# Two rounded TensorE products in place of an fp32 one for the partition sums of eight modulation blocks

## The chip, the core and the metric

The kernel runs on one core of a Trainium2 chip. The metric is the device time of one execution in microseconds (us); the median of several runs counts. TensorE is called PE below (PEld is its weight load), VectorE DVE, ScalarE ACT, GpSimd POOL; SP, the sync engine, only issues DMAs here.

## What is computed

A two-layer diffusion backbone over 2048 latent tokens and 256 context tokens, model width 1024. Every layer is modulated by a condition vector:

```python
def modulation(cond, w, b):
    m = jnp.dot(jax.nn.silu(cond), w) + b
    return jnp.split(m[..., None, :], 3, axis=-1)      # shift, scale, gate

for i in range(DEPTH):                                  # DEPTH = 2
    shift, scale, gate = modulation(c, ada_w[i], ada_b[i])
    c_shift, c_scale, c_gate = modulation(c_ctx, ada_w[i], ada_b[i])
    h = rms_norm(x, norm_g[i]) * (1 + scale) + shift
    hc = rms_norm(cx, norm_g[i]) * (1 + c_scale) + c_shift
    ...
```

Layer 0 is a latent attention beside a gated linear attention, layer 1 a neighbourhood attention. The modulation is a product of two condition vectors (latent and context) with a 1024 x 3072 matrix for each layer. Cut into columns of 512, that is six blocks for each layer: blocks 0 and 1 are the shift, 2 and 3 the scale, 4 and 5 the gate.

## The kernel before

**Numbers as pairs.** Most products on PE are of `float32r` operands. A value is split into a part `hi`, rounded to `float32r`, and the rest `lo`, and a product is three PE instructions: hi by hi, hi by lo, lo by hi (`mm3`). ACT makes `hi` by a copy, DVE makes `lo` by a subtraction.

**Stages.** `even_latent` runs over 18 tiles of 128 tokens. For tile `s` it normalises and modulates the input (`prep`: PE transposes L335 into the tile `px`, ACT scales them into `x`, DVE makes `hhi` and `hlo`), multiplies by three pieces of a weight matrix (`gemm`: W0, W1, W2, 24 PE instructions of 352 columns each, tile `gm`), and brings the result to SBUF as `u` (ACT). One tile later `up` transposes `u` on PE (L499, two groups of four into the tile `tp`), splits it into `lth` (ACT) and `ltl` (DVE), and makes queries, keys and values from it (`WU`, `wkv`). Another tile later `fin` transposes these (L554) and stores them. `even_rest` goes on with the remaining weight columns and row maxima of the attention scores, `even_mix` holds the attentions, `odd_*` is layer 1.

**The modulation.** `ada_first` makes blocks 0 to 3 of layer 0 at the start. The eight others (4 and 5 of layer 0, all six of layer 1) come from `ada_steps`, a generator that `even_latent` advances once for each tile from the third on, and twice at two tiles. For a block, DVE multiplies eight weight tiles `adaw` with the two conditions and adds them into the tiles `acc` (named `adac`, 128 x 512, one for each condition; L280 for the first weight tile, L282 for the other seven). The sum over the 128 partitions is then left to PE: at L287 an fp32 product with `pick`, a 128 x 2 matrix with a column of ones, puts the sum for condition `c` into row `c` of a PSUM tile `ps`. `ada_row` adds the bias on DVE (L296, into the tile `adab`) and, for the shift and scale of layer 1 (blocks 0 to 3), transposes the two rows with four small PE products (L301) into a second PSUM tile, from which DVE writes `modB` (L304) or `modA` (L306). Gates are stored to memory instead.

**Buffers.** The tag `adaw` has two SBUF buffers in `ada_steps`, so that a weight tile's DMA waits until DVE has read the tile before the last. `tp` has two PSUM banks; the modulation's two PSUM tiles share them with the transposes L499 and L554. `gm` and `u` have two buffers each.

**Order.** Each engine runs its instructions in a fixed order, written when the program is built: a scheduler places every instruction on its engine by its own estimate of when the operands are there. An instruction that waits holds up everything behind it on its engine. A small edit can thus move many instructions that it doesn't touch.

Of the kernel before, what the change touches and what calls it, by code (L numbers as in the profile page):

```python
# [11 lines left out]
F32R = mybir.dt.float32r  # L12
AF = mybir.ActivationFunctionType
ALU = mybir.AluOpType
# [3 lines left out]
P = 128  # L18
# [70 lines left out]
class Kern:  # L89
# [119 lines left out]
    def consts(self, es):  # L209
        nc = self.nc  # L210
        self.cp = self.pool(es, "const")
        cp = self.cp
        self.ident = self.tl(cp, [P, P], "ident")
        make_identity(nc, self.ident[:])
        self.mtwos = self.tl(cp, [P, 64], "mtwos")
        nc.gpsimd.memset(self.mtwos[:], -2.0)
        self.mhalf = self.tl(cp, [P, 8], "mhalf")
        nc.gpsimd.memset(self.mhalf[:], -0.5)
        self.ng = self.tl(cp, [P, 2, KD], "ng")
        nc.sync.dma_start(self.ng[:], self.i["norm_g"])  # L220
        self.modA = [self.tl(cp, [P, KD, 2], f"modA{l}") for l in range(2)]
        self.modB = [self.tl(cp, [P, KD, 2], f"modB{l}") for l in range(2)]
        self.condT = self.tl(cp, [P, KD, 2], "condT")
        cond = self.tl(cp, [P, KD, 2], "cond")
        nc.sync.dma_start(cond[:], self.i["cond"])
        th = self.tl(cp, [P, KD, 2], "condth")
        self.act(th[:], cond[:], AF.Tanh, scale=0.5)
        nc.vector.scalar_tensor_tensor(out=th[:], in0=th[:], scalar=1.0, in1=cond[:], op0=ALU.add, op1=ALU.mult)
        nc.vector.tensor_scalar(out=self.condT[:], in0=th[:], scalar1=0.5, scalar2=None, op0=ALU.mult)
        self.pick = self.tl(cp, [P, 2, 2], "pick")  # L230
        nc.gpsimd.memset(self.pick[:], 0.0)
        for c in range(2):
            nc.gpsimd.memset(self.pick[:, c, c : c + 1], 1.0)
        self.gates = self.scr("gates", (2, 2, D), F32)
        self.H = self.scr("H", (2, NT, P, D), F32)

# [33 lines left out]
    def ada_steps(self, jobs, sp, pp, tag):  # L270

        nc = self.nc
        for l, b in jobs:
            acc = [self.tl(sp, [P, 512], f"adac{c}", bufs=1) for c in range(2)]
            for k in range(KD):
                w = self.tl(sp, [P, 512], "adaw", bufs=2)
                nc.sync.dma_start(w[:], self.i["ada_w"][l, :, b, k, :])
                for c, a in enumerate(acc):
                    if k == 0:
                        nc.vector.tensor_scalar(out=a[:], in0=w[:], scalar1=self.condT[:, k, c : c + 1], scalar2=None, op0=ALU.mult)  # L280
                    else:
                        nc.vector.scalar_tensor_tensor(out=a[:], in0=w[:], scalar=self.condT[:, k, c : c + 1], in1=a[:],  # L282
                                                       op0=ALU.mult, op1=ALU.add)
            yield
            ps = self.tl(pp, [P, 512], tag, bufs=2)
            for c, a in enumerate(acc):
                nc.tensor.matmul(ps[:2, :], self.pick[:, c, :], a[:], start=c == 0, stop=c == 1)  # L287
            self.ada_row(l, b, ps, sp, pp, tag)
            yield

# [1591 lines left out]
```

## Time and profile before

| | us |
|---|---|
| runs | 3614.48, 3615.36, 3619.56 |
| median | 3615.36 |
| profiled execution | 3617.2 |
| its span, from the first to the last instruction | 3615.4 |
| mean granted PE clock | 0.988 |

The span is what the profile's views cover; the 1.8 us around it belong to no instruction. A group row of the profile reads: line, engine, operation, output <- inputs, shapes, count, then busy us and the mean ns of one, and the idle time of the engine just before them with what ended it. A row of the timeline reads: start us, duration us, engine, line, operation, and in brackets the idle time before it and what ended it. A row of the windows reads: from:to, length, then busy us and count of each engine, the granted PE clock as a share of full speed, the share of the DMA engines and GB/s.

### The profile page before, as it was taken

What the parts mean: (1) busy time and instruction counts of PE and PEld (TensorE: products, weight loads), DVE (VectorE), ACT (ScalarE), POOL (GpSimd) and SP (SyncE); (2) the same over time, 40 slices, a digit from 0 to 9 for tenths busy, and PEclk for the clock granted to TensorE, in tenths of its full rate; (3) what the DMA queues carried; (4) which work ended last, traced back from release to release, by engine and by line L of the source; (5) the groups of instructions that cost most, each with busy time, mean ns of one, the idle gap of its engine ahead of it and who ended that gap; (6) DMA issues with size and microseconds to landing.
All of it is one profiled execution on the core that took longest, in us unless ns stands there. A gap on an engine that the chain in (4) does not pass through costs nothing. (4 is left out here: it accounts for less than half of the span.)

```text
span 3615.4 us, 51630 instructions
## 1 busy us (share of the span) xinstructions
PE 3523.6 (97%) x18260; PEld 2734.3 (76%) x18260; DVE 2372.3 (66%) x4876; ACT 1430.5 (40%) x2705; POOL 1212.6 (34%) x1342
## 2 busy tenths in 40 slices
PE   8999999999999999999999999999999999999899
PEld 6988998888886666656667878888788886555577
DVE  4677665888886776787664345444587874667721
ACT  5544551111115555555653134444422223555510
POOL 1433430111011232212312233333334444677743
PEclk9999999999999999999999999999999999999999
DMA  7555463222233343334534544456643437888654
GB/s 253 149 153 159 141 191 99 87 77 84 75 109 89 83 104 83 94 92 129 163 91 143 162 164 127 145 143 199 212 139 123 139 122 202 213 213 222 185 178 146
DMA packets 396683, 513.62 MB, mean 142 GB/s; under 512 B 61229, under 2 KB 275197, under 8 KB 390522
## 3 DMA queue, kind: packets, MB, share of 16 engines
q1 hardware_dynamic: 353242, 418.68, 40.0%
q0 software_dynamic: 20192, 56.97, 5.6%
q10 hardware_dynamic: 22992, 34.68, 2.8%
q8 instruction: 145, 2.38, 0.3%
q14 instruction: 112, 0.92, 0.1%
HBM read 330.61 MB, written 179.59 MB: 141 GB/s over the span
## 5 line engine op out<-in xcount | busy, mean ns | idle before, releaser
L1007 DVE TENSOR_TENSOR acc<-acc,apt 128x512 f32<-128x512 f32 x512 | 376.4, 764 | 150.6 <-ACT apt L106 147.0
L666 DVE TENSOR_REDUCE mm<-mx 128x1 f32<-128x512 f32 (+1 forms) x656 | 392.7, 627 | 90.6 <-PE mx L665 82.3
L106 ACT ACTIVATE apt<-st 128x512 f32<-128x512 f32 (+1 forms) x592 | 342.9, 593 | 269.0 <-PE st L1018 229.5
L958 PE MATMUL av<-apt,av 128*64 128x512 f32 (+1 forms) x1184 | 269.2, 592 | 0.0
L1016 PE MATMUL st<-aq,akh 97*128 97x512 f32 x576 | 246.8, 428 | 0.2 <-ACT apt L106 0.2
L665 PE MATMUL mx<-mk,mq 96*128 96x512 f32 (+1 forms) x656 | 238.5, 372 | 0.0
L1017 PE MATMUL st<-aq,akh 96*128 96x512 f32 x576 | 229.1, 398 | 0.0
L1018 PE MATMUL st<-aq,akl 96*128 96x512 f32 x576 | 228.5, 397 | 0.0
L1450 DVE CUSTOM_DVE_ANT_1 mx<-mx,mtab 128x465 f32<-128x465 f32 (+14 forms) x576 | 183.9, 338 | 47.2 <-PE mx L1444 34.5
L106 ACT ACTIVATE u<-gm 128x352 f32<-128x352 f32 (+1 forms) x144 | 70.3, 495 | 358.5 <-PE gm L131 207.7
L106 ACT ACTIVATE opt<-opt 128x930 f32<-128x930 f32 (+9 forms) x144 | 119.2, 830 | 234.5 <-POOL opt L1748 137.0
L958 PEld LDWEIGHTS av<-apt,av 128*64 128x64 f32 x1184 | 79.9, 137 | 152.0 <-issue 150.0
L1708 DVE TENSOR_TENSOR opt<-st,tab 128x64 f32<-128x64 f32 (+10 forms) x576 | 143.0, 314 | 78.3 <-PE st L1548 44.7
L1583 POOL TENSOR_TENSOR oacc<-oacc,opt 128x682 f32<-128x682 f32 (+9 forms) x144 | 173.9, 1230 | 37.8 <-ACT opt L106 36.6
L1016 PEld LDWEIGHTS st<-aq,akh 97*128 97x128 f32 x576 | 109.0, 189 | 72.7 <-issue 44.2
L665 PEld LDWEIGHTS mx<-mk,mq 96*128 96x128 f32 x656 | 122.7, 188 | 11.7
L1018 PEld LDWEIGHTS st<-aq,akl 96*128 96x128 f32 x576 | 110.2, 191 | 25.5
L1017 PEld LDWEIGHTS st<-aq,akh 96*128 96x128 f32 x576 | 110.6, 192 | 17.8
L106 ACT ACTIVATE x<-px,modB,modA 128x128 f32<-128x128 f32 x272 | 99.1, 468 | 58.5 <-PE px L335 39.5
L1547 PE MATMUL st<-q,kt 128*128 128x480 f32 (+5 forms) x256 | 98.7, 388 | 20.2 <-DVE opt L1708 14.8
L129 PE MATMUL gm<-w0h,hhi 128*128 128x512 f32 x288 | 115.3, 400 | 2.3 <-DVE hhi L347 2.3
L129 PE MATMUL gm<-w1h,hhi 128*128 128x512 f32 x288 | 116.7, 405 | 0.0
(584 smaller groups left out, 9906.5 us busy)
## 6 DMA issues: line engine op xcount, KB each, us to landing
q<-Q SPq DMA_DIRECT2D x48, 512.0 KB
H<-x ACTq DMA_DIRECT2D x36, 512.0 KB
adaw<-ada_w SPq DMA_DIRECT2D x64, 256.0 KB
x<-H SPq DMA_DIRECT2D x32, 512.0 KB
K1t<-okt POOLq DMA_DIRECT2D x32, 512.0 KB, 6.7
kt<-K1t SPq DMA_DIRECT2D x32, 512.0 KB
mtab<-rpb_q SPq DMA_DIRECT2D x16, 899.0 KB
QT<-qkhl SPq DMA_DIRECT2D x36, 384.0 KB
```

The source lines that it names most:

```text
L106: return self.nc.scalar.activation(out, in_, func, **kw)
L129: self.nc.tensor.matmul(out, lh(k), rh(k), start=j == 0, stop=False)
L665: mm = nc.tensor.matmul(ps[:, :w], q[:A_QK, (t % 6) * P : (t % 6) * P + P], k[:A_QK, k0 : k0 + w], start=True, stop=True)
L666: nc.vector.tensor_reduce(out=m[:, t, n : n + 1], in_=ps[:, :w], axis=AX.X, op=ALU.max)
L958: nc.tensor.matmul(O[j, nb][i * 64 : i * 64 + 64, :w], V[j, kt // TT][:, kt % TT, i * 64 : i * 64 + 64], pts[i][:, :w], start=n == 0, stop ...
L1007: self.add = nc.vector.tensor_tensor(out=acc[i][:, :w], in0=a[:, :w], in1=pts[i][:, :w], op=ALU.add)
L1016: nc.tensor.matmul(ps[:, :w], kh[: A_QK + 1, i, kq], qh[: A_QK + 1, :w], start=True, stop=False)
L1017: nc.tensor.matmul(ps[:, :w], kh[:A_QK, i, kq], ql[:A_QK, :w], start=False, stop=False)
L1018: mm = nc.tensor.matmul(ps[:, :w], kl[:A_QK, i, kq], qh[:A_QK, :w], start=False, stop=True)
L1450: nc.vector.tensor_tensor_reduce(out=s, in0=s, in1=tb[:, ri : ri + rn, ci : ci + cn], scale=1.0, scalar=-3e38, op0=ALU.add, op1=ALU.max, a ...
L1583: self.psum = nc.gpsimd.tensor_tensor(out=a, in0=a, in1=pts[:, :, a0 - r0 : a1 - r0, :], op=ALU.add)
L1708: nc.vector.tensor_tensor(out=pt[:, d[0], d[1]], in0=ps[:, d[0], d[1]], in1=tabs[j][i][:, ri : ri + rn, ci : ci + cn], op=ALU.add)
```

## The change

A `float32r` copy of `pick` is made at the start by ACT. For each of the two accumulated tiles of a block, ACT copies the values into a `float32r` tile `hi`, DVE subtracts to get the rest `lo`, and two `float32r` products with `pickr`, one of `hi` and one of `lo`, take the place of the fp32 product. The four products of a block add up in the same PSUM tile as before. `hi` and `lo` take the tag `adaw` and so its two buffers: for a block, `hi` and `lo` of condition 0 take both, and those of condition 1 take them again.

```diff
@@ consts
             nc.gpsimd.memset(self.pick[:, c, c : c + 1], 1.0)
+        self.pickr = self.tl(cp, [P, 2, 2], "pickr", F32R)
+        self.act(self.pickr[:], self.pick[:])
@@ ada_steps
             ps = self.tl(pp, [P, 512], tag, bufs=2)
             for c, a in enumerate(acc):
-                nc.tensor.matmul(ps[:2, :], self.pick[:, c, :], a[:], start=c == 0, stop=c == 1)
+                hi, lo = [self.tl(sp, [P, 512], "adaw", F32R, bufs=2) for _ in range(2)]
+                self.act(hi[:], a[:])
+                nc.vector.tensor_tensor(out=lo[:], in0=a[:], in1=hi[:], op=ALU.subtract)
+                nc.tensor.matmul(ps[:2, :], self.pickr[:, c, :], hi[:], start=c == 0, stop=False)
+                nc.tensor.matmul(ps[:2, :], self.pickr[:, c, :], lo[:], start=False, stop=c == 1)
             self.ada_row(l, b, ps, sp, pp, tag)
```

## The prediction

> **What bounds the kernel now.** I read the page first, then the busy time by stretches, then what PE waits for in the stretch where the eight blocks lie, then the timeline around single instructions. The page:
>
> ```profile
> span 3615.4 us, 51630 instructions
> PE 3523.6 (97%) x18260; PEld 2734.3 (76%) x18260; DVE 2372.3 (66%) x4876; ACT 1430.5 (40%) x2705; POOL 1212.6 (34%) x1342
> ```
>
> PE is busy for 97% of the span. The instructions of L287, the partition sums, lie between 119.7 and 445.3 us, and the windows show that PE is as busy there and less so just behind:
>
> ```profile
> L287 PE MATMUL tp<-adac,pick x32: 591/592/593, 119.7 to 445.3; 128*2 128x512 f32 x32
> ...
> 110.00:450.00 340.00, 332.26 (x2006) 304.62 (x2005) 248.17 (x468) 174.94 (x427) 137.14 (x254) 0.99 0.52 152
> 450.00:533.50 83.50, 80.18 (x494) 76.62 (x492) 56.30 (x102) 48.10 (x97) 29.23 (x44) 1.00 0.61 178
> 533.50:561.00 27.50, 23.12 (x115) 20.32 (x116) 8.31 (x13) 8.52 (x12) 1.34 (x2) 0.93 0.87 234
> ```
>
> PE is idle for 7.7 of the 340 us, DVE is busy for 73%, ACT for 51%. So in this stretch a microsecond of PE work that goes away is a microsecond of time, unless PE comes to wait. What it waits for now is nearly always DVE:
>
> ```profile
> PE up L122 <- DVE ltl L502: 4.0, 5, 1.8
> PE tp L499 <- DVE modA L306: 2.0, 1, 2.0
> PE tp L554 <- DVE qkhl L561: 0.9, 1, 0.9
> ```
>
> **The PE work of a block.** The timeline at the first block:
>
> ```profile
> 119.44 0.33 PE L122 MATMUL gm<-W1h,hlo 128*128 128x352 f32 x1
> 119.69 1.88 PE L287 MATMUL tp<-adac,pick 128*2 128x512 f32 x4
> 121.50 0.44 PE L499 MATMUL tp<-ident,u 128*128 128x128 f32 x2
> ```
>
> Durations of PE overlap, so starts are what counts. Two fp32 products are recorded as four passes. A 352-column product makes way for the next after 0.16 us (start to start in a row of them), so without the sums L499 could have started at 119.60; it starts at 121.50. The sums take 1.90 us. Their replacement is four float32r products over 512 columns, for which the products with `wkv` are the row: they follow each other at (191.54 - 191.07) / 2 = 0.235 us.
>
> ```profile
> 191.07 0.39 PE L120 MATMUL up<-wkvh,lth 128*128 128x512 f32 x1
> 191.30 0.39 PE L121 MATMUL up<-wkvl,lth 128*128 128x512 f32 x1
> 191.54 0.39 PE L122 MATMUL up<-wkvh,ltl 128*128 128x512 f32 x1
> ```
>
> 4 x 0.235 = 0.94 us, a saving of 0.96 a block and 8 x 0.96 = **7.7 us** in all. Bounds: a loss of as much as the sums take now, 8 x 1.90 = 15.2 us, if the doubled number of products ran at the fp32 pace of 0.95; a saving of 15.2 if they cost nothing. I take the row, which has the same operand type and moving size.
>
> **The work it adds elsewhere.** For each block two ACT copies and two DVE subtractions of 128 x 512:
>
> ```profile
> L348 DVE TENSOR_TENSOR hlo<-x,hhi 128x512 fp32r<-128x512 f32 x26 | 17.8, 684 | 0.2
> L106 ACT ACTIVATE lth<-tp 128x512 fp32r<-128x512 f32 x25 | 14.9, 598 | 30.7 <-PE tp L499 30.6
> ```
>
> 16 x 0.684 = 10.9 us on DVE and 16 x 0.598 = 9.6 us on ACT, with 92 and 165 us free in the stretch. As load that is hidden by PE's products; if all of DVE's share came out as waits, it would cost 10.9. What matters is the order. `hi` and `lo` of condition 0 come in time: the sums are not placed when the accumulation ends but long after. In the third block the last accumulation ends at 194.93 + 1.42 = 196.35 and the sums start at 202.19, a slack of 5.8 us against 0.60 + 0.68 needed.
>
> ```profile
> 194.93 1.42 DVE L282 SCALAR_TENSOR_TENSOR adac<-adaw,condT,adac 128x512 f32<-128x512 f32 x2 [0.43 <-DMA adaw<-ada_w]
> 202.19 1.88 PE L287 MATMUL tp<-adac,pick 128*2 128x512 f32 x4
> ```
>
> The second pair is different. `hi` and `lo` of condition 1 overwrite the buffers of condition 0, so they wait for PE's first two products, and PE's third and fourth wait for them. With free engines that chain is 0.39 (a product's duration) + 0.60 + 0.68 = 1.67 us. In the changed program's order PE has between the pairs some 28 instructions in the first block, 20 to 30 in the second, fourth, seventh and eighth (over 3.5 us at 0.16 each), which covers it. In the third the pairs are torn apart and covered as well. In the fifth and sixth block it has only eight products, 1.3 us, and in the sixth half of a tile's transposes besides. Behind the waiting instructions stand, on ACT, the copies of `lth` and `u`, and on DVE `hlo`, the bias L296 and `modA`: the next tile's inputs. The next block's weight DMA waits for the same buffers, with SP's later loads and stores behind it; at the fifth block it follows at once.
>
> Fifth block: in the new order the transposes of a tile (px) stand right ahead of the first pair, and on ACT the eight scalings of that tile stand ahead of `hi` of condition 1. The same work before:
>
> ```profile
> 341.04 1.09 PE L335 MATMUL px<-ident,x 128*128 128x128 f32 x8
> 341.74 2.90 ACT L106 ACTIVATE x<-px,modB,modA 128x128 f32<-128x128 f32 x8
> 341.89 0.41 PE L122 MATMUL gm<-W1h,hlo 128*128 128x352 f32 x1
> 342.44 0.67 DVE L296 TENSOR_TENSOR adab<-tp,adab 2x512 f32<-2x512 f32 x1
> ```
>
> Counted from the start of px, ACT is through at 0.70 + 2.90 = 3.60, `hi` at 4.20, `lo` at 4.88. PE reaches the fourth product at 0.85 (px) + 0.47 + 1.28 + 0.235 = 2.84: a wait of 2.0 us. L301 stands directly behind it and needs the bias: DVE has `hlo` (0.68) and L296 (0.67) to do first, so L301 can start at 6.23, and PE, held up, is there at 5.08: another 1.15. Together 3.2 us. The sixth block, with half the scalings ahead of `hi`, comes to 2.5 us by the same count. These waits stand in place of ones that are there now in the same tiles (0.91, and 1.95 with 0.26 behind it):
>
> ```profile
> 90.97 0.44 PE L120 MATMUL up<-WUh,lth 128*128 128x384 f32 x1 [1.08 <-ACT lth L106]
> 216.84 0.45 PE L122 MATMUL up<-WUh,ltl 128*128 128x384 f32 x1 [1.79 <-DVE ltl L502]
> 320.34 0.44 PE L122 MATMUL up<-WUh,ltl 128*128 128x384 f32 x1 [0.91 <-DVE ltl L502]
> 348.06 0.66 PE L499 MATMUL tp<-ident,u 128*128 128x128 f32 x4 [1.95 <-DVE modA L306]
> 349.75 0.66 PE L120 MATMUL gm<-W2h,hhi 128*128 128x352 f32 x1 [0.26 <-ACT u L106]
> ```
>
> Net: +2.3 for the fifth, +0.3 for the sixth. At the third block's tile the new order puts the products of W2 between `lth` and `ltl`, so that the 1.79 goes and about 0.5 for L301 and `lth` comes: -1.3. For two further tiles the new order has the first `up` product right behind the transposes of `u`, as the tile at 90.97 has now, which waited 1.08 for `lth`: +2.2. Sum of new waits **+3.5 us**.
>
> A wait costs more than its length when PE's clock falls. After the 1.95 us above:
>
> ```profile
> 348.00:350.00 2.00, 1.69 (x9) 1.29 (x10) 2.00 (x5) 1.25 (x3) 0.00 (x0) 0.80 0.47 130
> 350.00:352.00 2.00, 2.00 (x8) 2.00 (x9) 2.00 (x4) 0.06 (x1) 0.00 (x0) 0.50 0.80 215
> 352.00:354.00 2.00, 2.00 (x12) 2.00 (x12) 1.59 (x3) 0.00 (x0) 0.00 (x0) 0.85 0.70 234
> ```
>
> The granted clock is 0.80, 0.50 and 0.85 over three stretches of 2 us: 0.4 + 1.0 + 0.3 = 1.7 us lost. The sixth block had this already; I add **+1.7** once, for the fifth. The Trainium skill ("TensorE: Matmul & The Clock Gate", Part 1) has the clock fall to half only after an idle window of about 3.4 us. The trace differs: 1.95 us were enough. By the page the fifth block's pieces would cost no clock and the time would be 1.7 us lower, 3614 us; as far as the trace bears it out that case has a quarter of my forecast's chance below, 0.10, and lies inside its range.
>
> **The end of the stretch.** What is saved must get past two joints at which PE waits for something other than its own work:
>
> ```profile
> 533.55 1.94 PE L554 MATMUL px<-ident,kn 128*96 128x128 f32 x8 [3.33 <-POOL kn L541]
> 557.83 1.06 ACT L106 ACTIVATE wr1h<-wraw 128x1024 fp32r<-128x1024 f32 x1 [12.28 <-DMA wraw<-w_rest]
> 560.06 0.68 DVE L632 SCALAR_TENSOR_TENSOR u<-u,gm 128x512 f32<-128x512 f32 x1
> 560.79 1.12 PE L638 MATMUL tp<-ident,u 128*128 128x128 f32 x4 [4.33 <-DVE u L632]
> ```
>
> The first is a chain from the last tile's `wkv` products over ACT, DVE and POOL. In the new order 15 `gm` products that stood behind those `wkv` products stand ahead of them: the chain starts 15 x 0.16 = 2.4 us later than the saving would have it, and PE's wait grows by as much: **+2.4**. The second joint is a weight DMA that lands at a fixed distance behind that chain. In the new order DVE splits two weight tiles rather than one ahead of L632 (1.2 us more), and PE does three products (0.6 us) ahead of L638 that it did behind: **+0.6**.
>
> Sum: -7.7 + 3.5 + 1.7 + 2.4 + 0.6 = **+0.5 us**. The profiled execution of 3617.2 (span 3615.4 and 1.8 around it) would become 3617.7; the median stands 1.8 below its profiled execution, so I forecast **3616 us**. Beyond some 650 us the two programs have the same order but for neighbours swapped on DVE. The copy of `pick` at the start lies beside ACT's wait for the first loads.
>
> **The rivals.** (1) *The saving arrives.* If ACT and DVE run ahead of the order's estimate, as they did by 5.8 us at the third block, the waits at the fifth and sixth are no longer than those they replace, and if the `wkv` chain is as much shorter as it starts later, the joints take nothing. Then it is -7.7 and -1.3 for the wait of 1.79: 3606 us. For it: PE waits for only 7.7 of 340 us now. Against it: the eight ACT scalings ahead of `hi` are fixed by the order. (2) *The second pair's chain decides (slower).* Each of the four blocks with L301 behind them (third to sixth) waits as the fifth does, 3.2 us with 1.7 us of clock: 4 x 4.9 = 19.6, less what such waits take there now (1.79 + 0.91 + 1.95 and 1.7 of clock, 6.35), with the two further tiles (2.2), the joints (3.0) and the saving: 19.6 - 6.4 + 2.2 + 3.0 - 7.7 = +10.7, 3626 us. It decides as soon as more than two blocks have less than 1.67 us of PE work between their pairs when ACT and DVE get there. For it: DVE's queue has POOL-dependent work ahead of `lo` in the third and fourth block. Against it: 3.5 us and more of cover in the order there. (3) *The change doesn't do what it says:* with a two-column `pickr` the products might keep the fp32 pace, four of 0.95 in place of two. Then 15.2 us are lost where I have 7.7 saved: 3616 + 22.9 = 3639 us. Nothing in the trace has two columns in float32r; every float32r product in it runs at the pace above.
>
> **How the numbers follow.** 0.2%, about what a measurement of this kernel can tell from no change, is 7.2 us. Chances: my forecast 0.41, with its own range 3609 to 3622; rival 1 0.25; rival 2 0.31; rival 3 0.03. Within 0.2%: most of the forecast's, 0.38; faster: rival 1 and a little of the forecast's edge, 0.26; slower: 0.36. The range for 8 in 10 reaches from just below rival 1 to somewhat above rival 2: 3605 to 3630.
>
> **What would show it.** L287's successors should have 32 records of some 0.39 us in place of 32 of 0.59, starts 0.235 apart where they stand together. PE's idle time in the stretch should grow from 7.7 us, with waits named by the new `adaw` tiles or L301 at the fifth and sixth block only, and a clock below 0.9 there. The wait for `kn` should be near 5.7 us in place of 3.33. If those waits are absent and the first product of `even_rest` comes 7 us earlier, rival 1 holds; if waits on `adaw` stand at four or more blocks, rival 2; if the new products are more than 0.3 us apart, rival 3. I am wrong if the difference arises beyond 650 us.

## The result, and the profile after

| | before | after |
|---|---|---|
| median of 4 runs each, us | 3617.46 | 3637.58 |
| lowest and highest | 3614.48 to 3621.46 | 3635.64 to 3641.53 |
| span of the profiled execution | 3615.4 | 3633.8 |

After over before is 1.0054, with a 95% interval of 1.0041 to 1.0067: about 20 us slower. The forecast of 3616 us, no change to speak of, was wrong, and the time lies outside its range (3605 to 3630).

The first two lines of the page and the windows of the changed kernel (columns as in the prediction: length, busy time and count of PE, PEld, DVE, ACT, POOL, then the granted clock):

```profile
span 3633.8 us, 51692 instructions
...
PE 3519.1 (97%) x18260; PEld 2738.1 (75%) x18260; DVE 2391.4 (66%) x4892; ACT 1438.3 (40%) x2722; POOL 1210.6 (33%) x1342
```

```profile
110.00:450.00 340.00, 317.93 (x1942) 298.79 (x1940) 249.49 (x465) 175.94 (x427) 133.90 (x237) 0.98 0.51 147
450.00:533.50 83.50, 83.50 (x520) 80.35 (x519) 52.77 (x102) 47.31 (x102) 30.40 (x56) 1.00 0.55 160
533.50:561.00 27.50, 20.42 (x118) 19.03 (x117) 17.87 (x30) 12.85 (x20) 5.82 (x7) 0.88 0.89 248
```

PE is idle for 22.1 of the 340 us with the blocks, 7.7 before. Line numbers from 294 on are those of before plus 6. Two rows of the timeline show how far this has grown at the two joints:

```profile
547.18 1.92 PE L560 MATMUL px<-ident,kn 128*96 128x128 f32 x8 [6.96 <-DVE kn L546]
...
576.27 1.12 PE L644 MATMUL tp<-ident,u 128*128 128x128 f32 x4 [5.74 <-DVE u L638]
```

The first joint is 13.6 us later than before (533.55), the second 15.5 (560.79), the end 18.4. What PE waits for between 110 and 533 us in the changed kernel:

```profile
PE tp L293 <- DVE adaw L291: 3.9, 2, 2.7
PE tp L292 <- ACT adaw L106: 3.4, 2, 2.1
PE up L120 <- ACT lth L106: 2.8, 3, 1.6
PE px L341 <- DVE x L338: 2.5, 1, 2.5
PE gm L120 <- ACT u L106: 2.3, 4, 1.0
PE tp L307 <- DVE adab L302: 2.2, 3, 0.9
PE tp L505 <- DVE modB L310: 1.7, 1, 1.7
PE tp L505 <- DVE qkhl L567: 1.6, 1, 1.6
```

Only the first two name the splits, 7.3 us. The other waits come to 14.8 us, 2.2 of them for the bias and the rest for the tiles' other inputs; before, all waits in this stretch were 7.8. The sums themselves are what the prediction took them for. First block, timeline:

```profile
119.67 0.32 PE L122 MATMUL gm<-W1h,hlo 128*128 128x352 f32 x1
119.84 0.40 PE L292 MATMUL tp<-adaw,pickr 128*2 128x512 f32 x1
120.07 0.39 PE L293 MATMUL tp<-adaw,pickr 128*2 128x512 f32 x1
120.31 0.60 PE L505 MATMUL tp<-ident,u 128*128 128x128 f32 x4
```

The starts are 0.23 and 0.24 us apart (L505 is the transposes, L499 before).

**An account up to the first joint.** The position of the first joint is split into three: PE's idle time from 70 us on, the time lost to the clock (over windows of 2 us, PE's busy time times one minus the granted clock), and the remainder, which is PE's own work. Before: 533.55 = 14.5 idle + 5.9 clock + 513.2. After: 547.18 = 34.5 + 6.5 + 506.2. So PE's work is 7.0 us less, as foreseen, its idle time 20.0 more, the clock's share 0.6 more: together the 13.6. The same account is given for several of the runs below. Each is of one profiled execution, and executions of one kernel differ (the kernel before, beside the first runs: 3613.19 us at a mean clock of 0.989 to 3629.21 at 0.985), so a few us between two accounts prove little.

### The profile page after: what moved, and what is told of

It reads as the page before. It is cut to its first block, busy times and chain, and to the rows that moved or that the text cites. A ratio compares the mean times of both kernels' runs of the same rounds, so it can differ in the third digit from the quotient of the medians.

```text
span 3633.8 us, 51692 instructions
## 1 busy us (share of the span) xinstructions
PE 3519.1 (97%) x18260; PEld 2738.1 (75%) x18260; DVE 2391.4 (66%) x4892; ACT 1438.3 (40%) x2722; POOL 1210.6 (33%) x1342
## 5 line engine op out<-in xcount | busy, mean ns | idle before, releaser
L671 PEld LDWEIGHTS mx<-mk,mq 96*128 96x128 f32 x656 | 122.3, 188 | 11.2
```

The source lines that it names most:

```text
L671: mm = nc.tensor.matmul(ps[:, :w], q[:A_QK, (t % 6) * P : (t % 6) * P + P], k[:A_QK, k0 : k0 + w], start=True, stop=True)
```

## Which part of the change costs the time

A scheduler writes the order of all instructions anew with each edit, so an edit tried alone changes the order too. To part the two, the first runs fix the order. `impose` chains the instructions of each engine by edges that set only the order of issue; `ORDER` is a list of positions taken from the built program of one of the two kernels, and `spare` holds the instructions that the other program lacks, which the scheduler places; in the runs that keep `hi` in the weight buffers, the first two weight loads of each block are left to it as well. Each ratio below is to runs of the kernel before on the same chip and beside the run; microseconds are the ratio less one, times 3617.

```diff
+def impose(tc, nc, spare):
+    order = json.loads(zlib.decompress(base64.b85decode(ORDER)))
+    queue = {}
+    for i in nc.cur_bb.bb.instructions:
+        if not type(i).__name__.startswith("BassTile") and i.name not in spare:
+            queue.setdefault(str(i.engine).split(".")[-1], []).append(i)
...
+            if was is not None:
+                tc.add_manual_dep(ins, was.name, how, reason="order")
```

**Order of after, instructions of before.** The kernel before with `impose` and the order of the changed kernel.

> The instructions of the kernel before (fp32 sums, no splits, no second product), put on each engine in the order of the changed kernel (its added instructions left out of the order). Theory O (the order is the cause): the waits of the changed kernel that name neither the splits nor the bias behind them stay, 13.1 us between 110 and 533 us where there are 7.7 now, with 2.0 more at 70 to 110 us and 5.0 more at the two joints: +12.5, 3630 us or more. Theory C (the chain of the second pair is the cause): without splits there is no chain, the time is that of before, 3617 (3613 to 3621). If both have a share: between 3621 and 3630.

1.0026 (1.0017 to 1.0036), some 9 us: between the two theories, so both may have a share. The first joint is at 542.80 = 21.5 idle + 5.3 clock + 516.0. The new order is a cost by itself, also without any split: at the fifth and sixth block PE waits 1.97 and 3.32 us for the bias (`adab`), at the first joint 6.57.

**Order of before, instructions of after.** The changed kernel with `impose` and the order of before.

> The changed kernel, with all instructions that the kernel before has too in the order of before; only the splits, the added products, and the first two weight loads of each block are left to the scheduler. The four products of a block stand next to each other, so that the chain of the second pair is as bare as it can be. Theory O: the saving of 7.7 us arrives less a little chain, 3610 to 3616. Theory C: each of the eight blocks waits for the chain, 8 x (1.67 - 0.24) = 11.4 us less the 7.7 saved, and the clock falls behind it in some: 3621 to 3632.

1.0043 (1.0030 to 1.0055), 15.6 us, at the upper end of what theory C gave. So the loss does not need the new order: in the old one the new instructions cost about as much (the intervals overlap). First joint at 549.35 = 31.9 + 8.8 + 508.6. The waits from 110 to 530 us (L298 and L300 are the two products of a condition, L314 the transposes of the bias):

```profile
PE tp L298 <- ACT adaw L110: 8.5, 8, 2.0
PE up L126 <- DVE ltl L515: 4.0, 5, 1.1
PE tp L314 <- DVE adab L309: 3.2, 2, 2.1
PE tp L300 <- DVE adaw L297: 3.2, 8, 0.7
```

The chain of the second pair, 8.5 + 3.2 = 11.7 us, is in sum the 11.4 that were worked out for it; a block has from 0.8 to 2.3 us rather than 1.4 each. But with the 7.7 saved it explains 4 of the 15.6 us.

**A buffer of its own for lo.**

```diff
-hi, lo = [self.tl(sp, [P, 512], "adaw", F32R, bufs=2) for _ in range(2)]
+hi = self.tl(sp, [P, 512], "adaw", F32R, bufs=2)
+lo = self.tl(sp, [P, 512], "adal", F32R, bufs=1)
```

> As the run in the order of before, with a buffer of its own for lo: hi of condition 1 no longer waits for a product, only lo does. Theory C: what is left of the chain is 0.39 + 0.68 - 0.24 = 0.83 us a block, 6.6 in eight, so 5 us less than the run with the shared buffers, 3616. Theory O: as that run, within 3 us. If the work added on ACT and DVE is what costs, this is no faster either, and both stand above 3625.

1.0032 (1.0020 to 1.0045): 4 us less, near the chain's count (5), though the two intervals overlap. And still 11.6 above before, where theory C had 3616 us.

**The high part alone.** No `lo` (the rest is left out), so no chain.

```diff
-                nc.vector.tensor_tensor(out=lo[:], in0=a[:], in1=hi[:], op=ALU.subtract)
...
+                nc.tensor.matmul(ps[:2, :], self.pickr[:, c, :], hi[:], start=c == 0, stop=c == 1)
```

> In the order of before, with the high part alone: one ACT copy and one float32r product for each condition; the rest is left out of the sum. No chain between the pairs is left (two buffers, two copies). The two products take 0.47 us where the sums take 1.90, 1.43 x 8 = 11.4 us less work for PE. If what PE saves reaches the end when no wait takes its place: 3606. If the joints (the wait for kn, the weight load behind it) keep it: 3613 to 3617. If the copy on ACT alone already costs (its place in ACT's queue), above 3618.

1.0023 (1.0014 to 1.0033): 8 us slower with 11.4 us less for PE and no chain. All expectations of a gain fail. The third alternative has the time, but not the reason: PE does not wait for ACT's copy once between 110 and 530 us, and waits 10.2 us for the bias. The timeline at the third block shows a wait that the prediction had named and not priced. First this kernel (L288 and L290 are the next block's accumulations, L306 the bias, L311 its transposes), then the same place before:

```profile
203.59 0.63 PE L297 MATMUL tp<-adaw,pickr 128*2 128x512 f32 x2
...
208.77 0.49 DVE L288 TENSOR_SCALAR adac<-adaw,condT 128x512 f32<-128x512 f32 x1 [1.95 <-DMA adaw<-ada_w]
...
211.22 0.75 DVE L290 SCALAR_TENSOR_TENSOR adac<-adaw,condT,adac 128x512 f32<-128x512 f32 x1 [1.96 <-DMA adaw<-ada_w]
211.89 0.67 DVE L306 TENSOR_TENSOR adab<-tp,adab 2x512 f32<-2x512 f32 x1
...
212.62 0.41 PE L311 MATMUL tp<-ident,adab 2*128 2x2 f32 x4 [4.07 <-DVE adab L306]
```

```profile
205.96 0.52 DVE L280 TENSOR_SCALAR adac<-adaw,condT 128x512 f32<-128x512 f32 x1 [0.64 <-DMA adaw<-ada_w]
206.60 0.75 DVE L282 SCALAR_TENSOR_TENSOR adac<-adaw,condT,adac 128x512 f32<-128x512 f32 x1
207.27 0.67 DVE L296 TENSOR_TENSOR adab<-tp,adab 2x512 f32<-2x512 f32 x1
...
208.52 0.41 PE L301 MATMUL tp<-ident,adab 2*128 2x2 f32 x4
```

DVE has two accumulations of the next block ahead of the bias. `hi` sits in the weight buffers until its product, so the next weights are fetched only then; DVE waits twice 1.95 us for them, the bias stands behind, and PE waits 4.07 us for the bias.

**Rounded accumulation: the cheap products and nothing else.** In the order of before, all engines. The values are accumulated in `float32r` tiles, rounded at each step, and go to the product as they are.

```diff
-acc = [self.tl(sp, [P, 512], f"adac{c}", bufs=1) for c in range(2)]
+acc = [self.tl(sp, [P, 512], f"adac{c}", F32R, bufs=1) for c in range(2)]
...
-nc.tensor.matmul(ps[:2, :], self.pick[:, c, :], a[:], start=c == 0, stop=c == 1)
+nc.tensor.matmul(ps[:2, :], self.pickr[:, c, :], a[:], start=c == 0, stop=c == 1)
```

> All engines exactly in the order of before; the values are accumulated in float32r tiles by DVE, so that they are rounded at each step and need no split: one float32r product for each condition in place of an fp32 one, nothing added on ACT or DVE, nothing in the weight buffers. PE has 8 x (1.90 - 0.47) = 11.4 us less to do. Theory W (the weight buffers: hi and lo hold them, the next block's weights land some 3 us after the products, and DVE has their first multiplications ahead of the bias): nothing holds them here, the time falls, by 11.4 less what the bias at four blocks takes back (up to 1.4 each), 5.8 to 11.4 us below before. Theory K (PE's saving is not on the path in these tiles at all, whatever the buffers): within 3 us of before.

1.0003 (0.9994 to 1.0012): as theory K has it. The first joint is at 533.38 = 22.9 idle + 8.1 clock + 502.4. PE's work is 10.8 us less, as counted, and all of it is given back, 8.4 as idle time and 2.2 as clock. The waits from 110 to 530 us that grew (before: 0.2, 2.0, none and 0.4):

```profile
PE px L341 <- DVE x L338: 3.7, 3, 1.9
PE tp L505 <- DVE modA L312: 3.4, 1, 3.4
...
PE tp L307 <- DVE adab L302: 1.0, 1, 1.0
PE tp L505 <- DVE modB L310: 1.0, 1, 1.0
```

**Splits without the weight buffers.** In the order of before; `hi` has its own buffer, `lo` overwrites the (rounded) accumulated values.

```diff
+hi = self.tl(sp, [P, 512], "adah", F32R, bufs=1)
+self.act(hi[:], a[:])
+nc.vector.tensor_tensor(out=a[:], in0=a[:], in1=hi[:], op=ALU.subtract)
```

> In the order of before, with the splits and four products of the change, but without the weight buffers: hi has one buffer of its own, lo overwrites the accumulated values (float32r tiles, rounded at each step, which changes the values and no work). All four products stand together, so the chain is bare: hi of condition 1 waits for a product, then lo: 0.39 + 0.60 + 0.68 - 0.24 = 1.43 us a block, 11.4 in eight, less the 7.7 saved: about 4 us above before. Theory W: so, 10 us or more below the run in the order of before with the shared buffers (which stood 15.6 above before). If the chain and the added work cost it, not the buffers: no more than 4 us below that run, 12 to 16 above before.

1.0025 (1.0016 to 1.0034), 9 us above before. First joint at 540.37 = 25.7 + 8.2 + 506.5. The chain is as bare as in the run with the shared buffers and waits even longer for `hi`:

```profile
PE tp L296 <- ACT adah L110: 10.3, 8, 3.5
PE tp L298 <- DVE adac L295: 3.7, 8, 0.8
...
PE up L126 <- DVE ltl L513: 1.4, 2, 0.7
```

No wait for the bias is left in this list (3.2 us with the shared buffers). The difference between the two runs is 0.0018, 6.5 us: so much does holding the weight buffers cost, with an uncertainty, worked out from the two intervals, of some 1 to 12 us. That cannot tell theory W's 10 us or more from its alternative's 4 or less.

With these runs the 15.6 us of the change in the old order have their parts, as estimates: nothing from the saving, 9 from the splits and the two further products of each block, 6.5 from the weight buffers. Against the run with one product for each condition, the run with splits has 7.0 us more at the first joint: 4.1 of PE's work (16 x 0.235 = 3.8 were to be expected), 2.8 of waits, 0.1 of clock.

## Two versions in their own order

**Rounded accumulation,** the edit of before the last, without an imposed order.

> The same as the run with rounded accumulation, but in the order that the scheduler writes for it. If the order written anew costs by itself (9 us with the instructions of before in the order of the changed kernel): 5 to 12 us slower than that run in the order of before. If the order was bad only because it was made for late weights and a chain: within 3 us of it.

0.9995 (0.9984 to 1.0006): not to be told from before, nor from the imposed order. A new order need not cost anything; the first run's order had been written for other instructions. At the first joint this run's profile is 3.3 us ahead of before, 530.21 = 24.0 + 4.1 + 502.1, and the two other kernels below with the cheap products in the scheduler's own order are 2.4 (three weight buffers) and 4.3 us ahead (merged rotation). So a part of the saving may arrive there; the times of whole executions cannot tell 3 us from none.

**Columns in place of rows.** The four blocks with a shift or scale use the accumulated values as the stationary operand.

```diff
+                for j in range(4):
+                    q = slice(j * P, j * P + P)
+                    for c, a in enumerate(acc):
+                        nc.tensor.matmul(pt3[:, j, :], a[:, q], self.pick[:, c, :], start=c == 0, stop=False)
+                    nc.tensor.matmul(pt3[:, j, :], br[:, q], self.ident[:2, :2], start=False, stop=True)
```

> A rival to the change: in the four blocks with a shift or scale, the fp32 accumulated values are the stationary operand and pick the moving one (two columns), four pieces for each condition, and the bias is added by a third product into the same PSUM columns; the 2 x 512 row, its bias on DVE and the four transposes fall away. The two gate blocks of each layer stay as before. PE: 12 products of about 0.10 to 0.15 us (four of 2 columns take 0.41 at L301) in place of 1.90 + 0.41, so 0.5 to 1.1 us less a block, and no wait for a bias on DVE behind DVE's queue. In the scheduler's own new order: 2 to 8 us below before; if a new order costs 9 by itself, up to 5 above.

1.0019 (1.0008 to 1.0030), 7 us, against the first expectation and a little above the second's 5. The products were sized too low, and something else came with them. Timeline at the third block, and the windows there:

```profile
201.30 0.50 PE L293 MATMUL tp<-pick,adac 128*128 128x2 f32 x4
...
203.81 1.02 PE L293 MATMUL tp<-pick,adac 128*128 128x2 f32 x4
204.76 0.58 PE L294 MATMUL tp<-ident,adab 2*128 2x2 f32 x2
205.28 1.12 PE L523 MATMUL tp<-ident,u 128*128 128x128 f32 x4
```

```profile
202.00:204.00 2.00, 2.00 (x15) 1.92 (x15) 1.80 (x7) 0.11 (x1) 1.92 (x2) 0.90 0.92 345
204.00:206.00 2.00, 2.00 (x10) 1.97 (x11) 0.51 (x1) 1.34 (x3) 1.42 (x7) 0.50 1.09 328
```

The block takes 205.28 - 201.30 = 3.98 us in place of 1.90 + 0.41, its end at a falling clock; at the next block, at a clock of 1.00, one of the four pieces takes 256.67 - 255.82 = 0.85 us, 3.4 for four. The granted clock falls to 0.50 while PE is busy for all of the 2 us. In the account, 539.45 = 12.5 + 12.2 + 514.8: against before the clock costs 6.3 us more, PE's work 1.6 more, and the waits 2.0 less.

## What holds PE's saving

**The sums twice.** In the order of before, fp32 sums, each block's made a second time.

```diff
+for c, a in enumerate(acc):
+    nc.tensor.matmul(ps[:2, :], self.pick[:, c, :], a[:], start=c == 0, stop=c == 1)
```

> The kernel before in its own order, with the fp32 sums of each block made twice in place: 8 x 1.90 = 15.2 us more for PE, nothing else. If PE's own work sets the pace in these tiles: 15 us above before. If the chain over ACT, DVE and SP sets it (as the run with 11.4 us less of PE work and no gain suggests): the added work fills waits where there are any and shows only where PE had none to spare, 4 to 10 us above before.

1.0010 (0.9999 to 1.0020), 3.6 us, near the second alternative, and at the first joint 4.5: 538.03 = 10.8 + 2.1 + 525.1. From start to start (first block: 119.76 to 123.28 us, before 119.69 to 121.50) the second pass takes 3.52 - 1.81 = 1.71 us, 13.7 in eight blocks rather than 15.2. In the account 11.9 are found in the remainder, 3.7 us of PE's waits and 3.8 of the clock's losses go. So much of PE's work in these tiles is exchanged for its waits and for the clock that falls behind them, in both directions.

**DVE relieved,** the fp32 sums kept, in the order of before: condition 1 is accumulated over 8 columns.

```diff
+q = slice(0, 8 if c else 512)
-nc.vector.scalar_tensor_tensor(out=a[:], in0=w[:], ...
+nc.vector.scalar_tensor_tensor(out=a[:, q], in0=w[:, q], ...
```

> The kernel before in its own order, with DVE relieved: the seven accumulations of condition 1 in each block go over 8 columns in place of 512, the rest of that condition is left out. 56 x about 0.65 = 36 us less work for DVE, no instruction moved. If DVE's queue is what the tiles' chain waits for: the 11 us of PE's waits between 70 and 533 us fall to a few, and the clock drop at 348 us goes: 6 to 12 us below before. If the chain runs over the x load and ACT's scalings: within 3 us of before.

0.9980 (0.9970 to 0.9990), 7 us, within the 6 to 12 expected: what DVE does for the blocks does cost time.

**DVE relieved and cheap sums:** this edit and that of the rounded accumulation.

> Both: DVE relieved as in the run before this one (condition 1 accumulated over 8 columns only), and the sums as one float32r product of rounded accumulated values for each condition. If DVE's queue turned PE's saving into waits, it arrives now: 9 to 11 us below the run with DVE relieved alone. If not DVE: within 3 us of that run.

0.9977 (0.9966 to 0.9989): only 1 us further. DVE's accumulations alone do not hold PE's saving; that theory falls.

**Three weight buffers** with rounded accumulation, in its own order.

```diff
-w = self.tl(sp, [P, 512], "adaw", bufs=2)
+w = self.tl(sp, [P, 512], "adaw", bufs=3)
```

> Rounded accumulation with one float32r product for each condition (values rounded at each step), in the scheduler's own order, with three weight buffers in place of two, which lets a block's weights come one ahead. If the waits for weights on DVE (19.5 us of its idle time in before) reach PE: 4 to 8 us below before. If not: as the same kernel with two buffers, within 3 us of before.

0.9993 (0.9980 to 1.0006): the same as with two.

The wait for `x` in the run with the cheap products alone led to GpSimd. The timeline of that run at the fifth block's tile, then the same place before:

```profile
316.13 0.56 POOL L210 TENSOR_TENSOR ssx<-ssx,mhalf 128x1 f32<-128x1 f32 x1
316.72 0.75 DVE L338 TENSOR_SCALAR x<-x,ssx 128x1024 f32<-128x1024 f32 x1 [1.79 <-POOL ssx L210]
317.53 1.09 PE L341 MATMUL px<-ident,x 128*128 128x128 f32 x8 [1.91 <-DVE x L338]
```

```profile
314.37 0.56 POOL L206 TENSOR_TENSOR ssx<-ssx,mhalf 128x1 f32<-128x1 f32 x1
314.96 0.75 DVE L332 TENSOR_SCALAR x<-x,ssx 128x1024 f32<-128x1024 f32 x1 [1.78 <-POOL ssx L206]
315.76 1.09 PE L335 MATMUL px<-ident,x 128*128 128x128 f32 x8
```

In both, DVE waits for GpSimd; before, PE comes to the transposes just when `x` is there, with cheaper sums it is there 1.91 us too early. That is early within the tile: with cheaper sums the tile's `u` is ready 1.3 us later than before (ACT writes it at 308.01 and at 306.69 us), from waits in tiles ahead of it.

**GpSimd relieved.** In the order of before, the key's rotation (four products of 128 x 8 a tile) left out.

```diff
+if z == 0:
     g.tensor_tensor(out=rot[:, :, o : o + 8], in0=x[:, :, s : s + 8], ...
```

> The kernel before in its own order, with the key's rotation (four products of 128x8 on GpSimd in each tile, 2.3 us) left out; nothing else changes place. Theory P (GpSimd's chain from u to x stands beside PE's work in each tile and is about as long, so that the shorter of the two does not count): with fp32 sums PE is there hardly earlier, the time falls little, 0 to 5 us below before. If GpSimd has no part: within 2 us of before.

0.9984 (0.9975 to 0.9994), 6 us, a little more than theory P's 0 to 5.

**GpSimd relieved and cheap sums:** again with the edit of the rounded accumulation.

> In the order of before, GpSimd's rotation left out as in the run before this one, and the sums as one float32r product of rounded accumulated values for each condition (11.4 us less for PE). Theory P: the waits of px for x (1.00, 0.76 and 1.91 us with the rotation) go, and 4 to 9 of the 11.4 us arrive beyond the run with the rotation left out alone. If another chain (ACT's scalings, modA and modB) holds it: no more than 2 us beyond that run.

0.9992 (0.9981 to 1.0002): no gain over the run before it, where theory P had 4 to 9 us. The three waits for `x` are still there (0.67, 0.76 and 1.26 us), and at the sixth block PE waits 3.49 us for `modA`, with a clock of 0.50 in the windows from 346 to 350 us. GpSimd's chain alone does not hold the saving either.

**The rotation in two instructions,** values kept, with fp32 sums and with cheap ones, each in its own order.

```diff
+for p in range(2):
+    g.tensor_tensor(out=four(rot[:])[:, :, :, p, :], in0=four(x[:])[:, :, :, 1 - p, :], in1=sj[:, :, :, p, :], op=ALU.mult)
```

> The kernel before with fp32 sums and all values kept; the rotation of queries and keys takes two instructions over both axes in place of four (on GpSimd some 1.1 us less a tile, on DVE 0.3), in the scheduler's own new order. Theory P: 0 to 5 us below before, plus or minus what the new order does (it did +9 with one order and -2 with another). If GpSimd has no part: the order alone, anywhere within 9 us.

> The merged rotation and the sums as one float32r product of rounded accumulated values, in the scheduler's own order. Theory P: GpSimd's chain is 1.1 us shorter in each tile, so that part of PE's saving arrives: 5 to 10 us below before. If not: as the run with rounded accumulation in its own order, 0 to 3 us below before.

1.0008 (0.9998 to 1.0018) and 1.0002 (0.9993 to 1.0011): no gain, in the second against its expectation.

**DVE and GpSimd relieved together,** in the order of before, with fp32 sums and with cheap ones.

> The kernel before in its own order, with both left out: condition 1's accumulations (8 columns in place of 512) and GpSimd's rotation of the key. With fp32 sums. The two alone gave 7.2 and 5.8 us; if they hold different tiles up: 11 to 14 us below before, if the same: 6 to 9.

> The same with the sums as one float32r product of rounded accumulated values for each condition, 11.4 us less for PE. If several chains of other engines about as long as PE's work took the saving: now it arrives in good part, 5 to 11 us below the run with both relieved and fp32 sums. If the chain that takes it runs over ACT's scalings, modA and modB (waits of 3.36 and 3.49 us for modA with the cheap sums where there were 1.95 and 0.93), or PE's work there does not count: within 3 us of that run.

0.9972 (0.9960 to 0.9984) and 0.9968 (0.9956 to 0.9981). The two reliefs together give 10 us (7 and 6 alone), between the two alternatives. But the cheap sums bring 1.4 us more: the 5 to 11 expected if these two engines' chains took the saving do not come. The account at the first joint: 518.75 = 7.1 idle + 0.5 clock + 511.2 with fp32 sums, 516.94 = 14.3 + 3.0 + 499.7 with cheap ones. PE's work is 11.5 us less, its idle time 7.2 and the clock's losses 2.5 more. The waits that come back are of about 1 us each, for `x` (0.76, 1.07), `ltl` (1.37), `u` (0.58) and `modA` (1.84).

So even with both relieved, other engines' results come so soon behind PE's that a block's saving, some 1.4 us, is mostly lost. Which chain holds it then is not shown, and was not tried: `modA` may point to ACT's eight scalings, `ltl` and `u` to the copies on ACT.

The profile of before shows as much without an experiment. Follow the work back from the first joint: on PE as long as it runs without a pause, and at each pause over to what ended the wait. After 110 us this chain runs over PE for 239 of 424 us only, though PE is busy for nearly all of them, and over the sums of three of the eight blocks, the first, the sixth and the eighth. With DVE or with GpSimd relieved it runs over five blocks' sums, with both over seven. At a block off the chain a cheaper sum can bring nothing to the joint; at one on it, no more than the distance to the next chain. None of the versions tried that leave nothing out is faster than the kernel before by more than can be measured.

## Why the prediction was wrong, step by step

- **"A microsecond of PE work that goes away is a microsecond of time, unless PE comes to wait."** This is the step that failed, in its condition. The saving was sized rightly (7.7; the account shows 7.0), but the prediction looked for new waits only where an instruction was added. The shorter sums make waits by themselves: with 11.4 us less and nothing added, 1.0003 (0.9994 to 1.0012), PE's idle time up by 8.4 us and the clock's loss by 2.2. PE's 97% showed that it seldom waited, not by how little the other engines came in time.
- **The second pair's chain.** At the fifth block 3.2 us were worked out and 1.32 + 1.18 + 0.80 + 0.25 = 3.55 came; the count by queues was nearly right there. At the sixth, 2.5 became 5.97:

```profile
355.35 0.63 ACT L106 ACTIVATE adaw<-adac 128x512 fp32r<-128x512 f32 x1
...
356.04 0.39 PE L292 MATMUL tp<-adaw,pickr 128*2 128x512 f32 x1 [2.06 <-ACT adaw L106]
...
356.70 0.35 DVE L478 TENSOR_SCALAR u<-u,ssl 128x256 f32<-128x256 f32 x1 [1.68 <-POOL ssl L206]
...
357.49 0.62 DVE L477 TENSOR_SCALAR u<-u,ssl 128x768 f32<-128x768 f32 x1 [0.44 <-POOL ssl L206]
...
358.02 0.42 DVE L353 CAST hhi<-x 128x512 fp32r<-128x512 f32 x1
358.36 0.69 DVE L291 TENSOR_TENSOR adaw<-adac,adaw 128x512 fp32r<-128x512 f32 x1
359.10 0.59 PE L293 MATMUL tp<-adaw,pickr 128*2 128x512 f32 x1 [2.67 <-DVE adaw L291]
```

  `hi` stood behind four scalings that began only at 353.98, since ACT was at the squares of `u` until then. `lo` stood on DVE behind the scaling of `u`, which waited twice for GpSimd, and behind `hhi`. The prediction counted from the start of px (351.36) with an ACT that was free 0.70 us later, and without that wait for GpSimd.
- **"The next block's weight DMA waits for the same buffers."** Named and given no price: about 6.5 us (1 to 12) in the order of before.
- **Net new waits of +3.5 us.** In the changed kernel, without the joint, 34.5 - 6.96 = 27.5 us of idle time stand against 14.5 - 3.33 = 11.2: +16.4. This is the term of the sum that was mis-sized. The fifth and sixth block have 9.5 of the 27.5 us where there were 3.1: +6.4 for the 2.6 forecast. Waits ahead of the first block have 5.5 for 3.4, and those at all other tiles 12.5 for 4.6: +7.9 where the forecast had -1.3 + 2.2 = +0.9. With the old instructions in the new order these others are 4.9 us, so most of the growth came with the new instructions; how much of them is the lost saving, the splits or the weight buffers was not measured in the new order. The "two further tiles" that wait for `lth` are there, with 1.61 and 0.91 us for the 2.2 expected.
- **The clock.** It fell at the fifth block as foreseen (0.56 and 0.58 in the windows from 328 to 332 us); up to the first joint the whole loss grew by 0.6 rather than 1.7 us, since other drops were smaller.
- **The joints.** The wait for `kn` grew from 3.33 to 6.96 (5.7 expected), the second from 4.33 to 5.74 (+1.4, not +0.6): together 2.0 us more than forecast.
- **Beyond 650 us.** 15.5 of the profile's 18.4 us are there at the second joint. From there to the end the profiles of the runs here take 3051.0 to 3066.4 us, so that the other 2.9 are within what varies there.
- **The rivals.** The second had the sign, at 3626. Its mechanism asked for waits on the splits at four blocks, and they came at two, as the forecast had it; it too lacked the buffers and the loss of the saving. The third had the time, 3639, by luck: its reason, the fp32 pace, did not occur (0.235 us a product).

## What to carry to other kernels

Where a fixed order has been laid out around an operation, the operation's time is also the other engines' time to get ready: before a saving on a busy engine is counted, follow the chain of work back through its waits, see which of the cheaper instructions lie on it, and look at how early the engine's next inputs come, tile by tile. Take as saved no more than that lead. A scratch tile that borrows another tile's buffers is paid for at that tile's next load and by all that stands behind its first use. And a change is best tried in both orders, its own and the old one: alone, neither of them tells the edit from the order.

## What was not expected of the hardware

The granted clock can fall while PE is busy without a break: in the version with columns, products of 2 columns with 128 x 128 weights ran from 201.30 us, and at 204 to 206 us the clock was 0.50 with PE busy for 2.00 of 2.00 us. The last wait before it had ended at 197.12. The clock fell at each of the four blocks made so (from windows at 202, 258, 312 and 340 us on, to 0.50 to 0.55), and at no other place between 100 and 538 us. The Trainium skill ("TensorE: Matmul & The Clock Gate", Part 1) has the clock go down after an idle window of some 3.4 us. The trace differs: in the 6 us ahead of the fall no idle time was recorded, as far as the modelled ends of PE's instructions tell. Why the clock falls there, no run shows.
